# RWKV time mixing: channel pairs transposed as float32 words between the matmuls of R, and a second weight pair

## The chip, the cores and the metric

The kernel runs on one core of a Trainium2 chip. The engines of a core run side by side and wait for each other through semaphores: TensorE (PE, with its weight loads shown apart as PEld), VectorE (DVE), ScalarE (ACT), GpSimd (POOL) and SyncE (SP), beside 16 DMA engines. The metric is the device time of one execution in microseconds (us): the median of several runs.

## The reference

x is 16 batches of 2048 tokens with 256 channels, all float32. Each token is mixed with the token before it, channel by channel, and projected:

```python
x_prev = np.zeros_like(x)
x_prev[:, 1:, :] = x[:, :-1, :].copy()
xv = x * time_mix_v + x_prev * (1 - time_mix_v)
xr = x * time_mix_r + x_prev * (1 - time_mix_r)
v = xv.reshape(-1, d_model) @ value_weight
r = xr.reshape(-1, d_model) @ receptance_weight
r_sigmoid = 1.0 / (1.0 + np.exp(-r))
out = (r_sigmoid * v).reshape(-1, d_model) @ output_weight
```

The key projection of the reference does not reach the output.

## The kernel before

The work is cut into 64 units of 512 tokens, four to a batch. A projection contracts over channels, so x must stand with channels on the 128 partitions: 256 channels make two halves (`ko`). For batches 0 to 9 (`STAGED`; units 0 to 39) TensorE makes that layout: x is loaded as bf16 into `x_bf` (unit 1, and unit 0, as float32 into `x_unit`), and `transposes` turns eight 128x128 blocks of a unit, four token slots by two halves, into one `ps_t` tile of PSUM, of which there are two. ACT copies the tile to `xt`. Batches 10 to 15 reach that layout by DMA transposes (the crossbar) out of a staged bf16 copy in DRAM, and need no work of TensorE for it.

The mixing is split between weights and data: a weight row is scaled by the mix (`tms`), and the data becomes `x + c * x_prev` with `c = 1 / mix - 1` (`c_sb`). The products with c are shared by DVE (`scale`), POOL (`scale_pool`) and ACT (`scale_act`); DVE adds x (`add`). The result is `mix`, with a part for r (m = 0) and one for v (m = 1). `coefficients` makes `tms` and `c_sb` at the start from one transpose of the mix rows.

The schedule is written out by hand. Iteration g of the main loop issues, in this order:

- R: four 512-column matmuls of unit g into `psum_r` (one buffer), by `project`; then ACT's sigmoid into `s_sb`.
- T: `advance` issues the transposes and ACT copies of a later unit, six ahead in the steady state; iterations 2, 5, 6 and 8 take two units (`START_T`). Eight transposes a unit.
- products and sums of later units on DVE; the last sum here releases POOL's product.
- V: four matmuls into `psum_v` (one buffer); DVE's product z = `s_sb` times `psum_v`, into `z_sb`.
- POOL's product (`scale_pool`), and DVE's sum for R of unit g + 2.
- O: eight matmuls of unit g − 1 into `psum_o` (one buffer), ACT's copy to the output tile, and the store.

Each engine takes its instructions in that order. What an iteration waits for are the single PSUM buffers: R for the sigmoid before, V for z before, O for the output copy before, and a transpose for the ACT copy that frees its `ps_t` tile, the tile of two units before. `w_bf` holds both scaled weights for all units; `w_f32` is their float32 source, loaded once at the start.

Of the kernel before, what the change touches and what calls it, by code (L numbers as in the profile page):

```python
# [1 line left out]

# [6 lines left out]
FP32 = mybir.dt.float32  # L9
# [6 lines left out]
def kernel(  # L16
# [47 lines left out]
    ZEROS_AT = 12  # L64
    SINGLE = NU - 6
# [99 lines left out]
    tm_rows = consts.tile([2 * KO, P], FP32)  # L165
    w_f32 = consts.tile([P, 2, KO, D], FP32)
    for m, tm in enumerate([time_mix_r, time_mix_v]):
        nc.scalar.dma_start(
            out=tm_rows[m * KO : (m + 1) * KO, :], in_=tm.rearrange("(ko p) -> ko p", p=P)
        )  # L170

    def load_halves(e):
# [8 lines left out]
        out=w_f32[:, 0], in_=receptance_weight.rearrange("(ko p) n -> p ko n", p=P)  # L181
    )
    load_halves(1)
    nc.sync.dma_start(out=w_f32[:, 1], in_=value_weight.rearrange("(ko p) n -> p ko n", p=P))
# [47 lines left out]
    tm_prev = consts.tile([P, 2, KO], FP32)  # L232

    def coefficients():
        ps = ps_o_pool.tile([P, 2, KO], FP32, name="psum_o")
        nc.tensor.transpose(
            out=ps.rearrange("p m k -> p (m k)"), in_=tm_rows, identity=ident_f[: 2 * KO, : 2 * KO]
        )
# [21 lines left out]
    def transposes(i):  # L260
# [10 lines left out]
        def one(ps, jj, ko, src, idn):  # L271
            nc.tensor.transpose(  # L272
                out=ps[:, jj], in_=src[:, jj, ko * P : (ko + 1) * P], identity=idn
            )

        if i == 1:
            for h in (1, 0):
                ps = ps_t_pool.tile([P, H, KO, P], FP32, name="ps_t")
                for jj in range(H):
                    for ko in range(KO):  # L280
                        one(ps[:, :, ko], jj, ko, x_unit[:, i, h * H : (h + 1) * H], ident_f)
                nc.scalar.copy(out=xt[b][:, j0 + h * H : j0 + (h + 1) * H], in_=ps)
            return
# [5 lines left out]
        nc.scalar.copy(out=xt[b][:, j0 : j0 + UJ], in_=ps)  # L289
        if i in SHIFT_ACT:  # L290
            j, n = (j0 - 1, UJ) if b < BYUNIT else (0, J)
            nc.scalar.copy(out=xt[b][:, j, :, 1:P], in_=xt[b][:, j + n, :, 0 : P - 1])
            shifted.append((b, e))

    def first_transposes():
        def part(lo, n, pool, name):
            ps = pool.tile([P, n, KO, P], FP32, name=name)
            for jj in range(n):
                for ko in range(KO):
                    nc.tensor.transpose(  # L300
                        out=ps[:, jj, ko],
                        in_=x_unit[:, 0, lo + jj, ko * P : (ko + 1) * P],
# [9 lines left out]
        part(1, 1, ps_o_pool, "psum_o")  # L312

# [36 lines left out]

    def scale(piece, kos=(0, 1)):
        b, m, _, _ = piece
        for ko in kos:
# [3 lines left out]
                scalar1=c_sb[:, m, ko : ko + 1],  # L357
# [4 lines left out]
    def scale_pool(piece, after):  # L362
# [4 lines left out]
            scalar1=c_sb[:, m, 1:2],  # L367
# [12 lines left out]
    def project(ps, g, m, lo=0, hi=TU):  # L380
        b, e = divmod(g, UB)
        for mo in range(KO):
            for ko in range(KO):
                nc.tensor.matmul(  # L384
                    out=ps[:, mo, :],
                    lhsT=w_bf[:, m, ko, mo * P : (mo + 1) * P],
# [3 lines left out]
                )  # L390

# [174 lines left out]
    def advance(limit):  # L566
        nonlocal tnext
        while tnext <= min(limit, NU - 1):
            b, e = divmod(tnext, UB)
            for n in LOADS.get((b, e), ()):  # L570
                loads[n] = load(n)
            if tnext < NU - BYDMA:
                transposes(tnext)
            tnext += 1

# [7 lines left out]
    first_transposes()  # L583
# [20 lines left out]
    )  # L604
    scale(pieces(0)[1])
# [43 lines left out]
    def scale_act(piece, kos):  # L649
        b, m, _, _ = piece  # L650
        for ko in kos:
# [4 lines left out]
                scale=c_sb[:, m, ko : ko + 1],  # L656
# [3 lines left out]
    for g in range(NU - 1):  # L660
        ps_r = ps_r_pool.tile([P, KO, TU], FP32, name="psum_r")
        if g == 0:
# [9 lines left out]
        nc.scalar.activation(out=s_sb, in_=ps_r, func=ACT.Sigmoid)  # L672
        advance(START_T[g] if g < len(START_T) else g + LOOK)
# [89 lines left out]
```

## Time and profile before

| what | value |
|---|---|
| median of 3 runs | 199.12 us (198.97 to 199.16) |
| span of the profiled execution | 197.1 us |
| granted TensorE clock, 12 to 180 us | 1.00 in every stretch asked for |
| units with PE transposes, of these with bf16 | 39 after the first, 38 |
| period of a unit with transposes, without | 3.05 us, 2.60 us |
| last bf16 transposes start at | 111.1 us |

The profile's span runs from the first to the last instruction of the program. The profiled execution's own time is not listed apart; what the runs' median has beyond the span, 2.0 us, lies outside the recorded instructions. A row of the timeline has the start, the time to the end of the last instruction merged into it, the engine, the source line, the operation with output and inputs, and the number of instructions. Matmuls overlap their ends with the next one, so distances between starts are what counts on PE.

### The profile page before, as it was taken

Reading aid. Unit: us, or ns where it says so; the run is one execution under the profiler, and the core shown is the slowest. Engines: PE = TensorE matmul, PEld = TensorE weight load, DVE = VectorE, ACT = ScalarE, POOL = GpSimd, SP = SyncE. Lnnn points to the kernel's source line nnn. Section 1 sums busy time; section 2 is a strip of 40 time slices with the busy share of each in tenths; the row PEclk is TensorE's granted clock in tenths of the full one; section 3 lists DMA queues with packets and bytes.
Section 4 is the critical chain, followed back from the end, with each engine's and each line's share of the span. In section 5 each row is a group of like instructions: output and inputs, shape, how many; then the busy total and the mean of one; then the engine's idle time right before and its main releaser. Section 6 shows DMA issues by size and latency. Waiting matters only on the chain.

```text
span 197.1 us, 3735 instructions
## 1 busy us (share of the span) xinstructions
PE 191.8 (97%) x1358; PEld 123.3 (63%) x1364; DVE 183.2 (93%) x286; ACT 177.2 (90%) x197; POOL 85.9 (44%) x117
## 2 busy tenths in 40 slices
PE   8999999999999999999999999999999999999992
PEld 3556676666666666666666666666666666666660
DVE  0999999999999999999999999999999999999962
ACT  3799899999999999999999999999999999999982
POOL 2745542443665635624334266444443444444200
PEclk9999999999999999999999999999999999999999
DMA  5999999999999999999999999999999999999875
GB/s 171 244 190 223 218 263 253 248 264 259 300 419 278 289 294 336 271 236 206 367 206 290 330 347 191 204 210 284 290 301 424 421 419 419 411 422 421 338 321 219
DMA packets 35465, 58.13 MB, mean 295 GB/s; under 512 B 26004, under 2 KB 27000, under 8 KB 30712
## 3 DMA queue, kind: packets, MB, share of 16 engines
q1 hardware_dynamic: 31792, 41.34, 59.8%
q0 software_dynamic: 3504, 16.44, 41.6%
q8 instruction: 10, 0.16, 0.3%
q10 hardware_dynamic: 152, 0.13, 0.2%
q14 instruction: 7, 0.06, 0.1%
HBM read 34.34 MB, written 39.90 MB: 377 GB/s over the span
## 4 chain that ended last, share of the span: by engine, by line
PE 93%; DMA 4%; issue 0%; SPq 0%; ACT 0%
PE psum_r L384 28%; PE psum_v L384 27%; PE psum_o L416 27%; PE ps_t L272 9%; DMA x_bf<-in_x_dram 2%; DMA w_f<-n_receptance_weight_dram 2%; PE ps_t L416 1%; SPq L174 0%; PE psum_v L416 0%; PE ps_t L384 0%; PE psum_r L416 0%; ACT x_bf L446 0%
## 5 line engine op out<-in xcount | busy, mean ns | idle before, releaser
L364 POOL TENSOR_SCALAR mix<-xt_both,c_sb 128x1024 bf16<-128x1024 bf16 (+1 forms) x55 | 61.1, 1110 | 85.6 <-DVE mix L376 82.4
L711 DVE TENSOR_TENSOR z_sb<-s_sb,psum_v 128x1024 bf16<-128x1024 bf16 (+1 forms) x64 | 76.7, 1200 | 2.2 <-PE psum_v L384 1.1
L376 DVE TENSOR_TENSOR mix<-mix,xt_both 128x1024 bf16<-128x1024 bf16 x112 | 76.8, 696 | 1.4
L384 PEld LDWEIGHTS <-w_bf 128*128 128x128 bf16 x512 | 48.5, 98 | 39.1 <-DVE mix L376 0.4
L672 ACT ACTIVATE s_sb<-psum_r 128x1024 bf16<-128x1024 f32 x63 | 65.3, 1036 | 6.2 <-PE psum_r L384 6.0
L384 PE MATMUL psum_v<-mix,w_bf 128*128 128x512 bf16 (+1 forms) x252 | 64.8, 378 | 0.2
L384 PE MATMUL psum_r<-mix,w_bf 128*128 128x512 bf16 x250 | 64.6, 379 | 0.2
L416 PE MATMUL psum_o<-wo_bf,z_sb 128*128 128x256 bf16 x486 | 63.2, 273 | 0.0
L416 PEld LDWEIGHTS <-z_sb 128*128 128x128 bf16 x512 | 51.9, 103 | 17.9 <-DVE z_sb L510 0.7
L471 ACT COPY o_sb<-psum_o 128x1024 f32<-128x1024 f32 x50 | 51.2, 1024 | 4.9 <-PE psum_o L416 4.9
L289 ACT COPY xt_both<-ps_t 128x1024 bf16<-128x1024 bf16 x32 | 32.9, 1039 | 0.0
L272 PEld LDWEIGHTS <-x_bf 128*128 128x128 bf16 x304 | 19.7, 98 | 8.6 <-DMA x_bf<-in_x_dram 1.1
L272 PE MATMUL ps_t<-ident,x_bf 128*128 128x128 bf16 x304 | 22.5, 219 | 0.3 <-DMA x_bf<-in_x_dram 0.3
L354 DVE TENSOR_SCALAR mix<-xt_both,c_sb 128x1024 bf16<-128x1024 bf16 (+1 forms) x47 | 21.3, 463 | 0.0
L652 ACT ACTIVATE mix<-xt_both,c_sb 128x1024 bf16<-128x1024 bf16 x14 | 16.3, 1163 | 0.0
L376 DVE TENSOR_TENSOR mix<-mix,xt_first 128x1024 bf16<-128x1024 bf16 x15 | 10.6, 714 | 0.1
L471 ACT COPY x_bf<-psum_o 128x1024 f32<-128x1024 f32 x10 | 10.2, 1016 | 0.0
L354 DVE TENSOR_SCALAR mix<-xt_first,c_sb 128x512 bf16<-128x512 bf16 x22 | 6.6, 352 | 0.2
L289 ACT COPY xt_first<-ps_t 128x1024 bf16<-128x1024 bf16 x6 | 6.1, 1042 | 0.2 <-PE ps_t L272 0.2
L557 POOL COPY xt_first<-xt_first 128x254 bf16<-128x254 bf16 x5 | 2.0, 392 | 7.2 <-DVE mix L376 5.7
L364 POOL TENSOR_SCALAR mix<-xt_first,c_sb 128x512 bf16<-128x512 bf16 x6 | 4.1, 685 | 1.5 <-DVE mix L376 1.0
L162 POOL DMA_DIRECT2D x_bf<-in_x_dram x8 | 4.7, 583 | 0.0
(68 smaller groups left out, 52.6 us busy)
## 6 DMA issues: line engine op xcount, KB each, us to landing
out_dram<-o_sb SPq DMA_DIRECT2D x25, 1024.0 KB, 11.6
x_bf<-in_x_dram POOLq DMA_DIRECT2D x8, 1024.0 KB, 14.8
x_natural<-in_x_dram POOLq DMA_DIRECT2D x4, 1024.0 KB, 11.8
out_dram<-x_bf SPq DMA_DIRECT2D x4, 1024.0 KB, 14.4
x_natural<-in_x_dram POOLq DMA_DIRECT2D x4, 512.0 KB, 12.6
out_dram<-x_bf SPq DMA_DIRECT2D x4, 512.0 KB, 4.2
x_bf<-in_x_dram POOLq DMA_DIRECT2D x6, 256.0 KB, 6.5
o_sb<-in_x_dram SPq DMA_DIRECT2D x4, 256.0 KB, 3.8
```

Source lines behind the costliest of these rows:

```text
L162: return nc.gpsimd.dma_start(out=x_bf[b], in_=rows(b), max_dma_last_dim=run)
L272: nc.tensor.transpose(out=ps[:, jj], in_=src[:, jj, ko * P : (ko + 1) * P], identity=idn)
L289: nc.scalar.copy(out=xt[b][:, j0 : j0 + UJ], in_=ps)
L354: nc.vector.tensor_scalar(out=mixed(piece, ko), in0=tokens(piece, 0, ko), scalar1=c_sb[:, m, ko : ko + 1], scalar2=None, op0=ALU.mult,)
L364: op = nc.gpsimd.tensor_scalar(out=mixed(piece, 1), in0=tokens(piece, 0, 1), scalar1=c_sb[:, m, 1:2], scalar2=1.0, op0=ALU.mult, op1=ALU.mult,
L376: return nc.vector.tensor_tensor(out=mixed(piece), in0=mixed(piece), in1=tokens(piece, 1), op=ALU.add)
L384: nc.tensor.matmul(out=ps[:, mo, :], lhsT=w_bf[:, m, ko, mo * P : (mo + 1) * P], rhs=mixed((b, m, e * TU + lo, e * TU + hi), ko), start=(k ...
L416: nc.tensor.matmul(out=ps[:, j, :], lhsT=slot[:, ko, j], rhs=wo_bf[:, ko, :], start=(ko == 0), stop=(ko == KO - 1),)
L471: nc.scalar.copy(out=o[:, j0 : j0 + UJ, :], in_=ps)
L652: nc.scalar.activation(out=mixed(piece, ko), in_=tokens(piece, 0, ko), func=ACT.Copy, scale=c_sb[:, m, ko : ko + 1],)
L672: nc.scalar.activation(out=s_sb, in_=ps_r, func=ACT.Sigmoid)
L711: nc.vector.tensor_tensor(out=z_sb[:, :, c : c + n], in0=s_sb[:, :, c : c + n], in1=ps_v[:, :, c : c + n], op=ALU.mult,)
```

## The change

A row of a bf16 token has 256 channels, which are 128 pairs of two bytes each; a pair is read as one float32 word. A transpose of words moves channel 2c to the even half of partition c and channel 2c + 1 beside it, so four float32 transposes do for a unit what eight bf16 ones did, and half `ko` now holds every second channel rather than 128 in a row. ACT's copy reads the two interleaved halves out of PSUM with a step. The weight rows are loaded in that order (`(p ko)` for `(ko p)`), and unit 0 and 1 are transposed with a step of two. The mix rows are transposed in two pieces.

The crossbar keeps the old channel order, so batches from 10 on need weights and coefficients in the old order: `tm_cross` is transposed and copied at the start, and at iteration 10 (`CROSS_AT`) POOL loads both weights again and makes `tms_cross` and `c_cross`, with the reciprocal on DVE. At iterations 20 to 23 POOL scales one weight half each into `w_cross`.

From iteration 3 on (`WEAVE`), the transposes of the later unit are issued between the matmuls of R, one behind each, or two where an iteration takes two units; ACT's copies still stand behind the sigmoid. The diff, cut to its core:

```diff
+    CROSS_AT = 10
+    WEAVE = 3
...
-        out=w_f32[:, 0], in_=receptance_weight.rearrange("(ko p) n -> p ko n", p=P)
+        out=w_f32[:, 0], in_=receptance_weight.rearrange("(p ko) n -> p ko n", p=P)
...
+    def mixes_by(order, pool, name):
+        ps = pool.tile([P, KO, 2], FP32, name=name)
+        rows = tm_rows.rearrange(order, k=KO)
+        for ko in range(KO):
+            nc.tensor.transpose(out=ps[:, ko], in_=rows[:, ko], identity=ident_f[:2, :2])
+        return ps.rearrange("p k m -> p m k")
+
+    def cross_coefficients():
+        nc.gpsimd.tensor_scalar(
+            out=tms_cross, in0=tm_cross, scalar1=0.0, scalar2=1e-30, op0=ALU.is_equal, op1=ALU.mult
+        )
+        nc.gpsimd.tensor_tensor(out=tms_cross, in0=tms_cross, in1=tm_cross, op=ALU.add)
+        nc.vector.reciprocal(c_cross, tms_cross)
+        nc.gpsimd.tensor_scalar(
+            out=c_cross, in0=c_cross, scalar1=-1.0, scalar2=1.0, op0=ALU.add, op1=ALU.mult
+        )
+
+    def load_cross_weights():
+        for m, w in enumerate([receptance_weight, value_weight]):
+            nc.gpsimd.dma_start(out=w_f32[:, m], in_=w.rearrange("(ko p) n -> p ko n", p=P))
...
-        ps = ps_t_pool.tile([P, UJ, KO, P], BF16, name="ps_t")
+        ps = ps_t_pool.tile([P, UJ, P], FP32, name="ps_t")
         src = x_first[:, e - 2] if b == 0 else x_bf[b][:, e * UJ : (e + 1) * UJ, :]
-        for jj in range(UJ):
-            for ko in range(KO):
-                one(ps[:, :, ko], jj, ko, src, ident)
-        nc.scalar.copy(out=xt[b][:, j0 : j0 + UJ], in_=ps)
+        words = src.bitcast(FP32)
+
+        def one(jj):
+            nc.tensor.transpose(out=ps[:, jj], in_=words[:, jj], identity=ident_f)
+
+        def evacuate():
+            nc.scalar.copy(
+                out=xt[b][:, j0 : j0 + UJ],
+                in_=ps.bitcast(BF16).rearrange("p j (c o) -> p j o c", o=KO),
+            )
...
-    def project(ps, g, m, lo=0, hi=TU):
+    def project(ps, g, m, lo=0, hi=TU, between=()):
         b, e = divmod(g, UB)
+        w = w_bf if b < STAGED else w_cross
+        between = list(between)
+        share = -(-len(between) // (KO * KO))
...
+                for one in between[:share]:
+                    one()
+                del between[:share]
...
+        limit = START_T[g] if g < len(START_T) else g + LOOK
+        between, ends = begin(limit) if g >= WEAVE else ([], [])
...
-            project(ps_r, g, 0)
+            project(ps_r, g, 0, between=between)
...
+        if g == CROSS_AT:
+            load_cross_weights()
+            cross_coefficients()
+        if CROSS_AT + 10 <= g < CROSS_AT + 10 + 2 * KO:
+            scale_cross_weight(g - CROSS_AT - 10)
```

How this moves the instructions, at three places. First PE, in an iteration of the steady state, from the last two matmuls of R on; LDWEIGHTS is a weight load, and a float32 transpose has its load in the same row. Before:

```order
L384 LDWEIGHTS w_bf
L384 MATMUL psum_r<-mix,w_bf 128x512
L384 LDWEIGHTS w_bf
L384 MATMUL psum_r<-mix,w_bf 128x512
L272 LDWEIGHTS x_bf
L272 MATMUL ps_t<-ident,x_bf 128x128
```

Now, the same place up to the first matmul of V:

```order
L435 LDWEIGHTS w_bf
L435 MATMUL psum_r<-mix,w_bf 128x512
L321 MATMUL ps_t<-ident_f,x_bf 128x128
L435 LDWEIGHTS w_bf
L435 MATMUL psum_r<-mix,w_bf 128x512
L321 MATMUL ps_t<-ident_f,x_bf 128x128
L435 LDWEIGHTS w_bf
L435 MATMUL psum_v<-mix,w_bf 128x512
```

One transpose stands behind each matmul of R, where eight, each with a load of its own, stood behind the fourth.

Second PE in iteration 6, which transposes units 10 and 11. The rows begin with the transposes behind R's first matmul and go to those behind the fourth; the waits are shown:

```order
L321 MATMUL ps_t<-ident_f,x_bf 128x128 [waits Activation_49]
L321 MATMUL ps_t<-ident_f,x_bf 128x128
L435 LDWEIGHTS w_bf
L435 MATMUL psum_r<-mix,w_bf 128x512
L321 MATMUL ps_t<-ident_f,x_bf 128x128 x2
L435 LDWEIGHTS w_bf
L435 MATMUL psum_r<-mix,w_bf 128x512
L321 MATMUL ps_t<-ident_f,x_bf 128x128 [waits Activation_49]
L321 MATMUL ps_t<-ident_f,x_bf 128x128
L435 LDWEIGHTS w_bf
L435 MATMUL psum_r<-mix,w_bf 128x512
```

Each unit's first transpose waits for the ACT copy of the tile two units before. Both waits stood behind the whole of R and now stand inside it, ahead of its last matmul.

Third POOL and DVE at iteration 10; `z_sb` is z, `mix` a product or a sum. DVE before, from z of iteration 10 to z of iteration 11:

```order
L711 TENSOR_TENSOR z_sb<-s_sb,psum_v 128x1024
L376 TENSOR_TENSOR mix<-mix,xt_both 128x1024
L354 TENSOR_SCALAR mix<-xt_both,c_sb 128x8x128
L376 TENSOR_TENSOR mix<-mix,xt_both 128x1024
L711 TENSOR_TENSOR z_sb<-s_sb,psum_v 128x1024
```

DVE now:

```order
L781 TENSOR_TENSOR z_sb<-s_sb,psum_v 128x1024 [waits PE_49,Activation_49]
L251 RECIPROCAL c_cross<-tms_cross 128x4 [waits Pool_49]
L424 TENSOR_TENSOR mix<-mix,xt_both 128x1024 [waits DVE_49]
L402 TENSOR_SCALAR mix<-xt_both,c_sb 128x8x128
L424 TENSOR_TENSOR mix<-mix,xt_both 128x1024 [waits DVE_49]
L781 TENSOR_TENSOR z_sb<-s_sb,psum_v 128x1024 [waits PE_49,Activation_49]
```

POOL now, from its product of iteration 10 to that of iteration 11, which followed each other directly before:

```order
L412 TENSOR_SCALAR mix<-xt_both,c_sb 128x8x128 [waits DVE_49]
L258 DMA w_f_100<-in_receptance_weight_dram 128x2x256
L258 DMA w_f_100<-in_value_weight_dram 128x2x256 [waits DMAHW7_49]
L247 TENSOR_SCALAR tms_cross<-tm_cross 128x4
L250 TENSOR_TENSOR tms_cross<-tms_cross,tm_cross 128x4 [waits Pool_49]
L252 TENSOR_SCALAR c_cross<-c_cross 128x4 [waits DVE_49]
L412 TENSOR_SCALAR mix<-xt_both,c_sb 128x8x128 [waits DVE_49,PE_49,Activation_49]
```

DVE has a reciprocal more, which waits for POOL's second small operation; that one stands behind two issues of DMAs and the product.

More of the change, by code (lines that the diff above doesn't have):

```diff
@@ L1 @@
 from contextlib import ExitStack
+from functools import partial
 import concourse.bass as bass
@@ L232, with scale_cross_weight @@
     tm_prev = consts.tile([P, 2, KO], FP32)
+    tm_cross = consts.tile([P, 2, KO], FP32)
+    tms_cross = consts.tile([P, 2, KO], FP32)
+    c_cross = consts.tile([P, 2, KO], FP32)
+    w_cross = consts.tile([P, 2, KO, D], BF16)
+    def mixes_by(order, pool, name):
[16 more added lines that the diff above has]
+            nc.gpsimd.dma_start(out=w_f32[:, m], in_=w.rearrange("(ko p) n -> p ko n", p=P))
+    def scale_cross_weight(n):
+        m, ko = divmod(n, KO)
+        nc.gpsimd.tensor_scalar(
+            out=halves(w_cross[:, m, ko, :]),
+            in0=apart(w_f32[:, m, ko, :]),
+            scalar1=tms_cross[:, m, ko : ko + 1],
+            scalar2=1.0,
+            op0=ALU.mult,
+            op1=ALU.mult,
+        )
     def coefficients():
[L235 to L238, printed above, removed]
+        ps = mixes_by("m (p k) -> m k p", ps_o_pool, "psum_o")
         tm = consts.tile([P, 2, KO], FP32)
@@ L312, in first_transposes @@
         part(1, 1, ps_o_pool, "psum_o")
+        return mixes_by("m (k p) -> m k p", ps_t_pool, "ps_t")
     def slots(piece, off=0):
@@ L366, in scale_pool @@
             in0=tokens(piece, 0, 1),
-            scalar1=c_sb[:, m, 1:2],
+            scalar1=coefficient(b, m, 1),
             scalar2=1.0,
@@ L564, with begin @@
     tnext = 1
-    def advance(limit):
+    def begin(limit):
         nonlocal tnext
+        between, ends = [], []
         while tnext <= min(limit, NU - 1):
@@ L572, in advance @@
             if tnext < NU - BYDMA:
-                transposes(tnext)
+                ones, end = transposes(tnext)
+                between += ones
+                ends += [end] if end else []
             tnext += 1
+        return between, ends
+    def advance(limit):
+        between, ends = begin(limit)
+        for step in between + ends:
+            step()
     def apart(row):
@@ L604 @@
     )
+    nc.scalar.copy(out=tm_cross, in_=cross)
     scale(pieces(0)[1])
@@ L655, in scale_act @@
                 func=ACT.Copy,
-                scale=c_sb[:, m, ko : ko + 1],
+                scale=coefficient(b, m, ko),
             )
@@ L669 @@
         else:
-            project(ps_r, g, 0)
+            project(ps_r, g, 0, between=between)
         s_sb = zpool.tile([P, KO, TU], BF16, name="s_sb")
         nc.scalar.activation(out=s_sb, in_=ps_r, func=ACT.Sigmoid)
-        advance(START_T[g] if g < len(START_T) else g + LOOK)
+        for end in ends:
+            end()
+        if g < WEAVE:
+            advance(limit)
         if g in T_AT:
```

41 lines of the change are left out of this document (22 added, 19 removed).

## The prediction

> **What bounds the kernel now.** I read first the busy shares and the chain that ended last, then the table by stretch of time, then the order of events inside one unit.
>
> ```profile
> PE 191.8 (97%) x1358; PEld 123.3 (63%) x1364; DVE 183.2 (93%) x286; ACT 177.2 (90%) x197; POOL 85.9 (44%) x117
> ...
> PE 93%; DMA 4%; issue 0%; SPq 0%; ACT 0%
> ```
>
> PE carries 93% of the chain. DVE and ACT are close behind, so the question for every edit is which of the three it touches. A share over the whole span hides the stages; the table by stretch shows the one with PE transposes (to 111 us):
>
> ```profile
> 60.00:84.00 24.00, 24.00 (x192) 15.84 (x190) 22.94 (x35) 22.37 (x25) 12.58 (x18) 1.00 1.02 295
> 84.00:110.00 26.00, 26.00 (x207) 17.09 (x206) 24.75 (x37) 24.37 (x27) 8.95 (x9) 1.00 1.11 262
> ```
>
> The columns after the length are PE, PEld, DVE, ACT, POOL. PE has no idle at all, at full clock (1.00); DVE is busy for 22.94 of 24.00. A delay put into PE here is never made up, and a saving on PE is worth having only until DVE ends last. One unit on PE:
>
> ```profile
> 62.00 1.03 PE L384 MATMUL psum_r<-mix,w_bf 128*128 128x512 bf16 x4
> 62.87 0.61 PE L272 MATMUL ps_t<-ident,x_bf 128*128 128x128 bf16 x8
> 63.31 1.03 PE L384 MATMUL psum_v<-mix,w_bf 128*128 128x512 bf16 x4
> 64.17 1.04 PE L416 MATMUL psum_o<-wo_bf,z_sb 128*128 128x256 bf16 x8
> 65.05 1.03 PE L384 MATMUL psum_r<-mix,w_bf 128*128 128x512 bf16 x4
> ```
>
> Start to start, R (psum_r) takes 0.87, the eight transposes T 0.44, V 0.86, O 0.88: a period of 3.05 us. Durations overlap, so I use starts only. The same unit on ACT:
>
> ```profile
> 62.20 1.01 ACT L471 COPY o_sb<-psum_o 128x1024 f32<-128x1024 f32 x1 [0.20 <-PE psum_o L416]
> 63.11 1.03 ACT L672 ACTIVATE s_sb<-psum_r 128x1024 bf16<-128x1024 f32 x1
> 64.03 1.02 ACT L289 COPY xt_both<-ps_t 128x1024 bf16<-128x1024 bf16 x1
> ```
>
> One ACT instruction follows another at 0.91. The output copy starts 0.20 after O's slot ends (62.00), so 0.20 is the step from PE to ACT.
>
> **The transposes.** 38 units trade eight bf16 transposes for four float32 ones. The trace has float32 transposes of the same form, on unit 1, at full clock. On PE and on PEld:
>
> ```profile
> 7.18 1.04 PE L272 MATMUL ps_t<-ident_f,o_sb 128*128 128x128 f32 x8
> 8.05 0.59 PE L398 MATMUL psum_r<-xt_first,w_prev 128*128 128x512 bf16 x2
> ```
>
> ```profile
> 6.96 1.01 PEld L272 LDWEIGHTS ps_t<-ident_f,o_sb 128*128 128x128 f32 x8
> 7.94 0.21 PEld L398 LDWEIGHTS <-w_prev 128*128 128x128 bf16 x2
> ```
>
> Eight take 8.05 − 7.18 = 0.87, or 0.109 each, against 0.44 / 8 = 0.055 for a bf16 one. So 4 × 0.109 = 0.436 replaces 0.445: a gain of about 0.01 a unit, 0.3 us over 38 units, as long as a woven one costs as much as one in a row. That is the point to settle. If 0.109 were the weight load, weaving would hide it behind a 512-column matmul. The boundaries speak against it. The first load starts at 6.96, a whole matmul before 7.18, and is hidden already. The last transpose is followed by a bf16 weight load (7.94), which a bf16 transpose hides in 0.055; yet the next matmul starts only at 8.05. With a matmul part of 0.055 the eight would have ended near 7.18 + 7 × 0.107 + 0.055 = 7.98. So the matmul itself takes 0.109, and a woven pair costs 0.216 + 0.109. **Term: −0.3** (−0.4 to −0.2).
>
> The Trainium skill, TensorE: Matmul & The Clock Gate, in the sections on LDWEIGHTS and on the weight-path modes, says that float32 weights get no fast load and that a load takes its columns over 1.2, about 107 ns for 128. By that rule alone the row of eight would be bound by its loads, and weaving would be worth 0.22 us a unit; the step from 7.94 to 8.05 does not agree with it. This is the first rival below.
>
> The reader of the words (ACT, bf16 pairs at a step of 4 bytes) has no row here. The output copy reads float32 at a step of 4 bytes, the present reader bf16 at 2, and both take 1.01 to 1.02; I take no change, and keep the other end, a doubled read (+0.9), for a rival.
>
> **The weave.** From unit 3 on, three of four transposes (six of eight where an iteration takes two units) stand ahead of R's last matmul. In the steady stage R's result comes 0.33 later and the sigmoid starts at 0.20 + 0.87 + 0.33 = 1.40 from the period's start; sigmoid and reader end at 1.40 + 2 × 0.91 = 3.22, and the next output copy is due at 3.04 + 0.20 = 3.24. It just closes, so the steady stage pays nothing; what a longer loop costs is the fourth rival. In the early stage ACT has four or five instructions in some iterations. PE and ACT at iterations 5 and 6:
>
> ```profile
> 23.99 1.03 PE L384 MATMUL psum_r<-mix,w_bf 128*128 128x512 bf16 x4
> ...
> 27.48 1.03 PE L384 MATMUL psum_r<-mix,w_bf 128*128 128x512 bf16 x4
> ```
>
> ```profile
> 25.10 1.03 ACT L672 ACTIVATE s_sb<-psum_r 128x1024 bf16<-128x1024 f32 x1
> 26.01 1.02 ACT L289 COPY xt_both<-ps_t 128x1024 bf16<-128x1024 bf16 x1
> 27.06 0.40 ACT L292 COPY xt_both<-xt_both 128x254 bf16<-128x254 bf16 x1
> 27.37 1.01 ACT L289 COPY xt_both<-ps_t 128x1024 bf16<-128x1024 bf16 x1
> 28.27 1.02 ACT L471 COPY o_sb<-psum_o 128x1024 f32<-128x1024 f32 x1
> ```
>
> In R of iteration 5 the last matmul now ends at 23.99 + 0.87 + 6 × 0.109 = 25.51, so the sigmoid starts at 25.71, not 25.10, and ACT was idle before it. All that follows on ACT is 0.61 later: the reader of unit 9 starts at 27.98 and ends at 28.99. With two ps_t buffers the first transpose of unit 11 waits for that reader. It now stands behind R's third matmul, at 27.48 + 3 × 0.216 + 4 × 0.109 = 28.57, and starts near 29.05: 0.5 us of idle PE, with V and O queued behind it. Carrying ACT on to iteration 10 at 0.91 each, nothing makes this up and little is added. **Term: +0.5** (0, if ACT's lag is swallowed, to 0.9, if a second buffer is caught as well).
>
> **The second weight pair.** At iteration 10 POOL gets, behind its product (scale_pool), two weight loads and two small operations; DVE's reciprocal waits for the second of these, and behind it on DVE stand the sum for R of iteration 12 and the product z of iteration 11. POOL at that place, what such issues cost it elsewhere, and a small POOL operation:
>
> ```profile
> 43.75 1.11 POOL L364 TENSOR_SCALAR mix<-xt_both,c_sb 128x1024 bf16<-128x1024 bf16 x1 [0.98 <-DVE mix L376]
> ```
>
> ```profile
> 79.70 1.11 POOL L364 TENSOR_SCALAR mix<-xt_both,c_sb 128x1024 bf16<-128x1024 bf16 x1 [0.98 <-DVE mix L376]
> 80.77 1.25 POOL L158 DMA_DIRECT2D x_natural<-in_x_dram  x2
> 82.89 1.11 POOL L364 TENSOR_SCALAR mix<-xt_both,c_sb 128x1024 bf16<-128x1024 bf16 x1 [0.87 <-DVE mix L376]
> ```
>
> ```profile
> L554 POOL COPY xt_first<-xt_first 128x2 bf16<-128x2 bf16 x5 | 1.6, 316 | 0.1
> ```
>
> The product ends its slot at 43.75 + 1.07 = 44.82, two issues bring it to about 46.0, two small operations of some 0.2 (0.1 to 0.3) to 46.4. DVE in the same stretch:
>
> ```profile
> 43.57 1.21 DVE L711 TENSOR_TENSOR z_sb<-s_sb,psum_v 128x1024 bf16<-128x1024 bf16 x1
> 44.70 0.70 DVE L376 TENSOR_TENSOR mix<-mix,xt_both 128x1024 bf16<-128x1024 bf16 x1
> ...
> 46.52 1.21 DVE L711 TENSOR_TENSOR z_sb<-s_sb,psum_v 128x1024 bf16<-128x1024 bf16 x1
> ```
>
> The sum that starts at 44.70 now waits to 46.4 plus a reciprocal of about 0.2: DVE loses 1.9 us. The z at 46.52 moves to 48.4 and ends at 49.6. V of the next iteration needs the one psum_v buffer back, as an earlier place shows, where V starts 0.05 after a late z (31.14 + 1.21 = 32.35):
>
> ```profile
> 31.14 1.21 DVE L711 TENSOR_TENSOR z_sb<-s_sb,psum_v 128x1024 bf16<-128x1024 bf16 x1
> ```
>
> ```profile
> 32.40 1.02 PE L384 MATMUL psum_v<-mix,w_bf 128*128 128x512 bf16 x4
> ```
>
> ```profile
> 48.08 1.03 PE L384 MATMUL psum_v<-mix,w_bf 128*128 128x512 bf16 x4
> ```
>
> So the V of 48.08 starts at 49.7. **Term: +1.6** (1.2 with the small operations at 0.1 and issues at 0.55, 2.0 with 0.3 and 0.63); the weave's half microsecond moves both engines and leaves it alone. What goes nowhere: the four weight products on POOL (iterations 20 to 23; estimated at half of a 128x1024 product, 0.55) fit into its idle of at least 0.87 before each product; without it each would cost DVE up to 0.5. The two extra loads, 0.5 MB, run 30 us ahead of their use.
>
> **The start.** Two extra tiny transposes ahead of the coefficients push R of unit 0 by 0.1 to 0.2. Behind it PE waits for a load anyway:
>
> ```profile
> 10.25 0.62 PE L272 MATMUL ps_t<-ident,x_bf 128*128 128x128 bf16 x8 [0.31 <-DMA x_bf<-in_x_dram]
> ```
>
> That load is issued when the first weight lands; the weight now comes in 2 KB pieces, with unknown sign. **Term: +0.1** (−0.3 to +0.4).
>
> **The sum.** −0.3 + 0.5 + 1.6 + 0.1 = +1.9. The profiled execution spans 197.1; the runs' median of 199.12 lies 2.0 above, lead-in that the change does not touch. I expect a span of 199.0 and a time of **201.0**; all terms at their low ends give 199.6, at their high ends 202.2.
>
> **Rivals.**
> 1. The woven transpose costs 0.055, the load having been the limit. PE's period falls to 2.82, but DVE then ends last: 3.05 × 22.94 / 24.00 = 2.91. Saved: 0.13 × 23 iterations (11 to 33) = 3.0; DVE's stall of 1.9 counts in full, weave and start add 0.3: about 198.3. It decides for the other side if a woven transpose takes under some 0.07. For it: nothing here weaves them. Against: the step to 8.05. Chance 0.10.
> 2. The reciprocal hardly bites: if the two load issues did not hold up the POOL operations behind them, the coefficients would be there at 45.3, DVE would lose 0.7 and V 0.4, in all 199.6 or, with the weave free too, 199.2. Against: in the rows above the issues are serial on POOL. Chance 0.12.
> 3. As forecast, 201.0: chance 0.70.
> 4. Reading every second bf16 is slower on ACT. The loop above takes 0.28 more without harm, since the output copy may run into the wait for the sigmoid; a doubled read (+0.9) gives 3 × 0.91 + 0.9 = 3.63 a unit against 3.04, some 17 us over 30 units: 218; half of that, a few microseconds. Chance 0.08.
>
> A measurement of this kernel tells changes over about 0.2% (0.4 us) from none. Faster takes most of rival 1: 0.08. Within 0.2%: the rest of 1 and half of 2: 0.08. Slower: 0.84. The range of 8 in 10 goes from 199.2, which leaves out rival 1, to 202.6, which leaves out rival 4 and takes in the unknown ends.
>
> **What would show it.** Right: R with its woven transposes still 1.30 from start to start of V; a gap on PE of about 1.6 us at V of iteration 12, with DVE's reciprocal waiting for POOL; a gap of about 0.5 in R of iteration 6; a period of 3.04 at 60 to 84 us. Wrong: a period of 2.9 there (rival 1), a DVE that waits under 1 us at the reciprocal (rival 2), or a reader clearly over 1.04 us (rival 4).

## The result and the profile after

| | median | runs | profiled execution | its span |
|---|---|---|---|---|
| before | 199.14 us (198.97 to 200.03) | 4 | not listed apart | 197.1 |
| changed | 201.75 us (201.22 to 201.89) | 4 | 201.22 | 199.4 |

The ratio is 1.0114, with a 95% interval of 1.0077 to 1.0151: slower by 2.6 us in the medians. The profiled execution of the change is its fastest one. Ratios and their intervals, here and below, leave out executions more than 1.5% above the fastest of their kernel; the medians do not.

Three places that the prediction spoke of. First the steady stage, in the table by stretches (per engine busy us and instructions, then granted clock, DMA share, GB/s), of the changed kernel:

```profile
60.00:84.00 24.00, 24.00 (x160) 16.94 (x159) 23.46 (x34) 22.59 (x25) 14.02 (x20) 1.00 1.03 300
```

PE is still busy without a break, with fewer instructions. The groups by line, of the same kernel:

```profile
L321 PE MATMUL ps_t<-ident_f,x_bf 128*128 128x128 f32 x152 | 37.6, 274 | 0.3 <-ACT xt_both L324 0.3
L324 ACT COPY xt_both<-ps_t 128x1024 bf16<-128x1024 bf16 x32 | 32.2, 1015 | 0.0
```

One woven R, at iteration 32, from its second matmul on, and what follows it, on the timeline of PE:

```profile
109.78 0.38 PE L435 MATMUL psum_r<-mix,w_bf 128*128 128x512 bf16 x1
110.00 0.27 PE L321 MATMUL ps_t<-ident_f,x_bf 128*128 128x128 f32 x1
110.11 0.38 PE L435 MATMUL psum_r<-mix,w_bf 128*128 128x512 bf16 x1
...
110.65 0.27 PE L321 MATMUL ps_t<-ident_f,x_bf 128*128 128x128 f32 x1
110.76 1.03 PE L435 MATMUL psum_v<-mix,w_bf 128*128 128x512 bf16 x4
111.92 0.38 PE L435 MATMUL psum_r<-mix,w_bf 128*128 128x512 bf16 x1
...
113.22 1.04 PE L470 MATMUL psum_o<-wo_bf,z_sb 128*128 128x256 bf16 x8
114.09 1.03 PE L435 MATMUL psum_v<-mix,w_bf 128*128 128x512 bf16 x4
114.96 1.03 PE L435 MATMUL psum_r<-mix,w_bf 128*128 128x512 bf16 x4
116.21 1.03 PE L470 MATMUL psum_o<-wo_bf,z_sb 128*128 128x256 bf16 x8 [0.22 <-ACT o_sb L525]
```

From a matmul of R to its transpose are 0.22 us, from there to the next matmul 0.11: a woven float32 transpose costs PE 0.11, and four of them (0.44) as much as the eight bf16 ones did (0.44). ACT reads the interleaved halves in 1015 ns, no slower than the 1039 ns of before. The rows from 110.76 on show something else, the end of the stage with transposes, where O moves from behind V to behind the next R. V's four matmuls take 0.87 of PE, so the next R could start at 111.63 and starts at 111.92; and O at 116.21 waits for ACT.

Second, iteration 6, on the timeline of PE:

```profile
28.12 0.38 PE L435 MATMUL psum_r<-mix,w_bf 128*128 128x512 bf16 x1
28.76 0.44 PE L321 MATMUL ps_t<-ident_f,x_bf 128*128 128x128 f32 x2 [0.26 <-ACT xt_both L324]
```

0.64 us lie between the starts instead of 0.22: the transposes wait for ACT to free a `ps_t` tile, and R, V and O stand behind them. Third, iteration 10, on the timelines of POOL and of DVE:

```profile
44.81 0.78 POOL L258 DMA_DIRECT2D w_f<-n_receptance_weight_dram  x1
45.59 0.73 POOL L258 DMA_DIRECT2D w_f<-in_value_weight_dram  x1
46.40 0.24 POOL L247 TENSOR_SCALAR tms_cross<-tm_cross 128x4 f32<-128x4 f32 x1
46.73 0.20 POOL L250 TENSOR_TENSOR tms_cross<-tms_cross,tm_cross 128x4 f32<-128x4 f32 x1
```

```profile
43.57 1.22 DVE L781 TENSOR_TENSOR z_sb<-s_sb,psum_v 128x1024 bf16<-128x1024 bf16 x1
46.96 0.18 DVE L251 RECIPROCAL c_cross<-tms_cross 128x4 f32<-128x4 f32 x1 [2.17 <-POOL tms_cross L250]
47.06 0.66 DVE L424 TENSOR_TENSOR mix<-mix,xt_both 128x1024 bf16<-128x1024 bf16 x1
...
48.76 1.21 DVE L781 TENSOR_TENSOR z_sb<-s_sb,psum_v 128x1024 bf16<-128x1024 bf16 x1
```

DVE's reciprocal waits 2.17 us behind two issues and two small operations of POOL. The z that started at 46.52 before starts at 48.76, and V of iteration 12, at 48.08 before, at 50.03.

Comparing the starts of R and V of each iteration in both profiles, the change is 0.27 ahead after the start, 0.27 behind after iteration 9, 1.95 behind at V of iteration 12, 1.75 behind at the end of the steady stage, 2.36 behind from iteration 35 on, and stays there. The spans differ by 2.3. The last matmuls of PE in the changed kernel, and the last stretch of its table before the end:

```profile
195.30 0.39 PE L470 MATMUL psum_o<-wo_bf,z_sb 128*128 128x256 bf16 x2
```

```profile
184.00:192.00 8.00, 8.00 (x54) 5.44 (x53) 7.68 (x12) 7.49 (x10) 1.60 (x2) 1.00 0.94 383
```

From the end of that row to the end of the span are 3.75 us; in the kernel before, whose last matmuls end at 193.33, they are 3.78. So far the account closes on PE, with one item, the 0.6 at iterations 32 to 35, that the prediction did not have. The experiments show that it is only half of the account.

### The profile page after: what moved, and what is told of

It reads as the page before. It is cut to its first block, busy times and chain, and to the rows that moved or that the text cites. A ratio compares the mean times of both kernels' runs of the same rounds, so it can differ in the third digit from the quotient of the medians.

```text
span 199.4 us, 3456 instructions
## 1 busy us (share of the span) xinstructions
PE 192.5 (97%) x1215; PEld 126.3 (63%) x1215; DVE 183.9 (92%) x287; ACT 178.0 (89%) x198; POOL 91.8 (46%) x126
## 4 chain that ended last, share of the span: by engine, by line
PE 86%; ACT 5%; DVE 4%; POOL 2%; issue 1%; POOLq 0%
PE psum_v L435 25%; PE psum_o L470 25%; PE psum_r L435 24%; PE ps_t L321 7%; ACT s_sb L739 2%; PE ps_t L205 2%; DVE mix L424 2%; ACT xt_both L324 1%; DVE z_sb L781 1%; PE ps_t L470 1%; ACT o_sb L525 1%; POOL mix L412 1%; POOL w_f L258 1%; DVE mix L402 1%; ACT xt_first L314 1%
## 5 line engine op out<-in xcount | busy, mean ns | idle before, releaser
L412 POOL TENSOR_SCALAR mix<-xt_both,c_sb 128x1024 bf16<-128x1024 bf16 (+1 forms) x31 | 34.3, 1106 | 46.6 <-DVE mix L424 41.6
L435 PEld LDWEIGHTS <-w_bf 128*128 128x128 bf16 x316 | 30.5, 98 | 25.4 <-DVE mix L424 2.5
L412 POOL TENSOR_SCALAR mix<-xt_both,c_cross 128x1024 bf16<-128x1024 bf16 x24 | 27.0, 1124 | 35.4 <-DVE mix L424 34.1
L435 PE MATMUL psum_v<-mix,w_bf 128*128 128x512 bf16 x160 | 41.1, 379 | 1.1 <-DVE z_sb L781 0.8
L321 PE MATMUL ps_t<-ident_f,x_bf 128*128 128x128 f32 x152 | 37.6, 274 | 0.3 <-ACT xt_both L324 0.3
L324 ACT COPY xt_both<-ps_t 128x1024 bf16<-128x1024 bf16 x32 | 32.2, 1015 | 0.0
L435 PEld LDWEIGHTS <-w_cross 128*128 128x128 bf16 x196 | 19.2, 98 | 16.9
L435 PE MATMUL psum_r<-mix,w_cross 128*128 128x512 bf16 x96 | 24.6, 379 | 0.0
L435 PE MATMUL psum_v<-mix,w_cross 128*128 128x512 bf16 (+1 forms) x96 | 24.2, 375 | 0.0
L321 PEld LDWEIGHTS ps_t<-ident_f,x_bf 128*128 128x128 f32 x152 | 20.9, 141 | 4.5 <-ACT xt_both L324 1.4
L717 ACT ACTIVATE mix<-xt_both,c_cross 128x1024 bf16<-128x1024 bf16 x12 | 13.9, 1162 | 0.0
L525 ACT COPY x_bf<-psum_o 128x1024 f32<-128x1024 f32 x10 | 10.2, 1015 | 0.0
```

Of the source, the lines that this page charges most:

```text
L321: nc.tensor.transpose(out=ps[:, jj], in_=words[:, jj], identity=ident_f)
L324: nc.scalar.copy(out=xt[b][:, j0 : j0 + UJ], in_=ps.bitcast(BF16).rearrange("p j (c o) -> p j o c", o=KO),)
L412: op = nc.gpsimd.tensor_scalar(out=mixed(piece, 1), in0=tokens(piece, 0, 1), scalar1=coefficient(b, m, 1), scalar2=1.0, op0=ALU.mult, op1= ...
L435: nc.tensor.matmul(out=ps[:, mo, :], lhsT=w[:, m, ko, mo * P : (mo + 1) * P], rhs=mixed((b, m, e * TU + lo, e * TU + hi), ko), start=(ko = ...
L525: nc.scalar.copy(out=o[:, j0 : j0 + UJ, :], in_=ps)
L717: nc.scalar.activation(out=mixed(piece, ko), in_=tokens(piece, 0, ko), func=ACT.Copy, scale=coefficient(b, m, ko),)
```

## Experiments

Each experiment was timed beside runs of the kernel before, whose medians were 199.06 to 199.20 us; the ratios are against those. "Late" is how much later than in the kernel before (190.32 us) the last unit's first sigmoid starts in the profiled execution, a measure of PE's lateness at the end. T1 and T2 are the two DMA transposes (`by_dma`, in iterations 27 and 39); their ends are those of their rows on SP's queue (the data land some 3 us later). The columns from "late" on are of one profiled execution each, the medians of all.

| kernel | median, us (runs) | ratio, 95% | late | T1 starts | T2 ends | span |
|---|---|---|---|---|---|---|
| before | 199.1 to 199.2 | 1 | 0 | 95.1 | 146.1 | 197.1 |
| changed | 201.75 (4) | 1.0114, 1.0077 to 1.0151 | 2.36 | 96.2 | 148.9 | 199.4 |
| recip_later | 202.03 (6) | 1.0118, 1.0070 to 1.0165 | 1.14 | 96.8 | 147.6 | 198.2 |
| no_weave | 201.70 (6) | 1.0117, 1.0070 to 1.0164 | 1.99 | 97.0 | 150.6 | 201.1 |
| both_undone | 201.38 (5) | 1.0117, 1.0072 to 1.0163 | 2.12 | 97.8 | 148.8 | 199.2 |
| coeff_first | 200.44 (12) | 1.0062, 1.0037 to 1.0088 | 1.52 | 97.7 | 148.6 | 198.6 |
| mix_late | 201.01 (6) | 1.0083, 1.0050 to 1.0117 | 2.02 | 96.9 | 149.6 | 200.2 |
| products_late | 200.47 (12) | 1.0060, 1.0030 to 1.0090 | 1.78 | 97.5 | 149.5 | 200.1 |
| both_late | 201.38 (12) | 1.0110, 1.0080 to 1.0139 | 2.19 | 96.7 | 148.9 | 199.3 |
| no_reload | 201.11 (12) | 1.0064, 1.0029 to 1.0098 | 1.46 | 95.7 | 149.0 | 199.6 |
| before_reload | 200.29 (12) | 1.0052, 1.0022 to 1.0082 | −0.13 | 96.2 | 148.2 | 198.8 |
| undone_no_reload | 200.76 (12) | 1.0067, 1.0038 to 1.0096 | 0.26 | 94.9 | 148.0 | 198.6 |
| shuffle | 201.08 (12) | 1.0071, 1.0035 to 1.0107 | – | – | – | – |
| before_wait | 201.83 (6) | 1.0139, 1.0095 to 1.0184 | 3.01 | 95.7 | 148.5 | 200.1 |

The profile of shuffle is not in the table; it is of an execution of 202.50, far above the median.

### Taking the two engine prices away

recip_later: the reciprocal alone moves to iteration 12, when POOL has long delivered.

```diff
-        nc.vector.reciprocal(c_cross, tms_cross)        # iteration 10
+        if g == CROSS_AT + 2:
+            cross_reciprocal()
```

> The reciprocal of the crossbar coefficients moves from iteration 10 to iteration 12; loads, weave and float32 transposes stay. Theory (the reciprocal's wait for POOL costs PE 1.6 to 1.7 us): about 1.7 us less than the changed kernel, near 200.0 us, no wait at the reciprocal, and no gap on PE at V of iteration 12. Rival (the delay is the extra POOL and DMA work, wherever the reciprocal stands): under 0.5 us less, near 201.5 us.

no_weave: the transposes stay float32, but stand behind R in a block, as before.

```diff
-    WEAVE = 3
+    WEAVE = NU
```

> The four float32 transposes of a unit stand in one block behind R, as the eight bf16 ones did before; all else as in the changed kernel. Theory (the weave costs about 0.5 us at iteration 6 and about 0.6 us where the transposing stage ends, and a transpose costs 0.109 us either way): about 1.1 us less than the changed kernel, near 200.6 us, with the period at 60 to 84 us unchanged at 3.04. Rival (weaving hides the float32 weight load): the period grows, by up to 0.2 us a unit, and the kernel is slower by several us.

both_undone: both edits.

> Reciprocal at iteration 12 and no weave: what is left of the change is the float32 transposes, the reader with a step, and the second weight pair. Theory: the two prices add, 2.8 us less than the changed kernel, 198.7 to 199.1 us, level with the kernel before or 0.3 to 0.5 under it. Rival (the float32 transposes or the reader with a step cost time of their own): it stays over 199.6 us.

coeff_first: the reciprocal stays in iteration 10, but POOL makes the small operations ahead of the two load issues.

```diff
         if g == CROSS_AT:
-            load_cross_weights()
             cross_coefficients()
+            load_cross_weights()
```

> At iteration 10 the coefficient operations are issued ahead of the two weight loads, so POOL reaches them 1.5 us earlier; the reciprocal stays at iteration 10. Theory (DVE waits for POOL's queue, and the two load issues are 1.5 of its 2.2 us): DVE's wait falls to about 0.7 us, and the kernel is about 1.4 us faster than the changed one, near 200.3 us. Rival (the wait is for the coefficient operations themselves or for the transposed mix rows): the wait stays near 2.2 us, and so does the time.

coeff_first did what the mechanism says: the reciprocal waits 0.70 instead of 2.17, PE ends 1.52 late, and the median is 1.3 under the change. The other three are misses. Their profiles show the waits gone as meant: recip_later has no wait of DVE at iteration 10, no_weave none at iteration 6 and a lateness that stays at 1.99 from iteration 31 to the end, without the step of 0.6. Yet all three have a median within 0.4 of the change. (The profiled execution of recip_later, 199.99, is the lowest of its six and lies where the theory put it; that of no_weave, 202.84, is the highest of its six. Of the others there is no profile.) For no_weave a part of the miss is PE's own: it is only 0.37 less late than in the change, not 1.1, because its start was 0.5 later and the reciprocal cost PE 1.99 instead of 1.68. Two more things stood out in the profiles. In both_undone nearly all of PE's lateness is there after two iterations (2.04 of 2.12): R of unit 0 ran at half speed, a matter of that execution's start (last section). And in no_weave the end does not follow PE; here are its last matmuls and the two transposes, on the timelines of PE and SP:

```profile
194.94 0.39 PE L470 MATMUL psum_o<-wo_bf,z_sb 128*128 128x256 bf16 x2
```

```profile
97.03 15.29 SPq L288 DMA_TRANSPOSE xt_both<-x_natural  x1
137.06 13.50 SPq L288 DMA_TRANSPOSE xt_both<-x_natural  x1
```

The kernel before ended 3.8 us behind PE's last work (193.3 to 197.1); this one 5.7 behind (195.3 to 201.1). What ended late were stores, which stand behind T2 in SP's queue; T2 ended 4.4 later than before.

### Three guesses at what is late besides PE

Base of all four is recip_later. mix_late takes the second pair's mix transposes out of the start; products_late lets POOL scale the second pair behind its load issues; both_late does both; no_reload leaves out the two extra loads, so that batches 10 to 15 get weights in the wrong order of channels.

```diff
-        return mixes_by("m (k p) -> m k p", ps_t_pool, "ps_t")    # end of first_transposes
+        if g == CROSS_AT - 3:                                     # mix_late
+            nc.scalar.copy(out=tm_cross, in_=mixes_by("m (k p) -> m k p", ps_t_pool, "ps_t"))
...
-        if CROSS_AT + 10 <= g < CROSS_AT + 10 + 2 * KO:
+        if CROSS_AT + 14 <= g < CROSS_AT + 14 + 2 * KO:           # products_late
...
-            load_cross_weights()                                  # no_reload
```

> Base: the change with its reciprocal moved to iteration 12 (202.03 us median, 199.99 in its profiled execution). Here also the two small float32 transposes of the second pair's mixes, and their copy, leave the start and stand behind iteration 7's woven transposes. Theory A (these transposes among the warm-up matmuls make the TensorE clock rise late, near 9 to 10 us instead of 5, in most executions, for 2 us): the median falls to 199.7-200.4, and in the profile the first pairs of R's matmuls take 0.6 us, not 1.06. Theory B (the second pair's products delay the loads in DRAM, and with them the DMA transposes and the last stores) and theory C (the 0.52 MB that the second pair's loads add are what costs): the median stays at 201.5-202.3.

> Same base (reciprocal at iteration 12); here POOL makes the second pair's four products in iterations 24 to 27 instead of 20 to 23, behind the loads into x_natural that it issues in iterations 22 and 23. Theory B: the first DMA transpose starts at 95.3-96.0 us (base 96.85 with PE 0.5 late; before 95.12) and the second at 134.0-134.6, and the median falls by 0.5-1.5 to 200.5-201.5. Theory A or C: loads move but the median stays at 201.5-202.3.

> Both moves on that base: mixes' transposes out of the start and the four products behind the loads. If A and B together are the whole excess of the base over the kernel before plus weaving's 0.5-1.1: 199.5-200.2 median. If C: not under 201.

> Same base (reciprocal at iteration 12) without the two loads that fetch the weights a second time (the products then scale the rows in the order they were first loaded in, so that batches 10 to 15 are projected with channels in a wrong order). Theory C (their 0.52 MB and POOL's 1.5 us of issuing): the median falls to 199.7-200.5. Theories A and B: it stays at 201.5-202.3, perhaps 0.3 less.

mix_late fell to 201.01, not into the range of theory A, and its profile shows a price of its own: the small transposes take a `ps_t` tile at iteration 7, and PE comes out of iteration 8 some 0.6 later. both_late carries the same price, so its 201.38 beside products_late's 200.47 gives theory A no support; with intervals this wide neither run refutes it. products_late has a median that fits theory B, but not for B's reason: T1 starts at 97.5, no earlier than in the base. no_reload starts T1 at 95.7, 1.2 earlier than the base, as theory C says of the loads, but its time is well above C's range. No single guess explains it. In three of these profiles, though, the span follows T2's end: 149.6 and 200.2, 149.5 and 200.1, 149.0 and 199.6, with PE 2.02, 1.78 and 1.46 late.

### The DMA engines' price alone, and PE's price alone

before_reload is the kernel before with nothing of the change but the two loads, into a tile that nobody reads any more.

```diff
+        if g == 10:
+            for m, w in enumerate([receptance_weight, value_weight]):
+                nc.gpsimd.dma_start(out=w_f32[:, m], in_=w.rearrange("(ko p) n -> p ko n", p=P))
```

> The kernel before, with nothing of the change but the two loads that fetch the weights a second time (0.52 MB, on POOL's queue at iteration 10, into a tile that nothing reads any more). Theory D (the 16 DMA engines are busy without a pause to 184 us, and the first DMA transpose, the second and the last stores follow one another in this traffic; the two loads take 1.1 to 1.5 us of every engine): the first DMA transpose starts at 96.2-96.8 us instead of 95.1, the second ends at 147.3-148.0 instead of 146.1, and the median is 199.9-200.8. Theory of the prediction (only engines that wait for the loads pay): 199.1-199.4, both transposes as before.

This run separates the two best. The transposes on the timeline of SP, of the kernel before and of before_reload:

```profile
95.12 15.38 SPq L254 DMA_TRANSPOSE xt_both<-x_natural  x1
133.82 12.33 SPq L254 DMA_TRANSPOSE xt_both<-x_natural  x1
```

```profile
96.17 15.17 SPq L254 DMA_TRANSPOSE xt_both<-x_natural  x1
134.67 13.54 SPq L254 DMA_TRANSPOSE xt_both<-x_natural  x1
```

PE's last matmuls, in the same order:

```profile
192.94 0.39 PE L416 MATMUL psum_o<-wo_bf,z_sb 128*128 128x256 bf16 x2
```

```profile
192.82 0.39 PE L416 MATMUL psum_o<-wo_bf,z_sb 128*128 128x256 bf16 x2
```

PE is 0.12 early, T1 starts 1.05 late, T2 ends 2.1 late, the span is 1.6 longer and the median 1.2 higher; the interval of the ratio makes that 0.4 to 1.6. T1 and T2 each start 0.1 to 0.2 after the landing of the last load that feeds them. For T1 that load is issued at 81.33 and lands at 95.00 before; with the two extra loads it is issued at 81.23 and lands at 95.98. Of T2's 2.1, though, only 0.85 is its start; 1.2 is its length, and T2 is as long in profiles without the loads (13.3 in undone_no_reload, 13.2 in before_wait). That the loads lengthen it is not shown. T1's start is the clear sign: 94.9 to 95.7 in the four profiles without the loads, 96.2 to 97.8 in the nine with them.

Why half a megabyte matters shows in the table by stretches, first before (its row for 60 to 84 us is in the prediction) and then before_reload:

```profile
184.00:192.00 8.00, 8.00 (x57) 5.65 (x55) 6.42 (x9) 7.27 (x12) 0.89 (x1) 1.00 0.77 314
```

```profile
184.00:192.00 8.00, 8.00 (x58) 5.69 (x57) 6.30 (x9) 7.28 (x12) 0.77 (x1) 1.00 1.01 415
```

From 12 to 184 us the DMA share is 1.0 or above in every stretch, in both kernels. The kernel before has room in it only at the start (0.82 in the first 12 us) and in its last 13 us: 0.77 from 184 to 192. With the two loads the share is 1.01 there, and the stores drain until the end. The loads' half megabyte is 30 us ahead of its use, as the prediction said, but no stretch between shows a lower share in which it could hide. The share alone would not prove that: it can pass 1 (1.18 from 130 to 150 us in before_reload), so it counts some time twice. What shows it is the run.

The Trainium skill, "DMA: Bandwidth & Descriptors", section "Issuing engines are not separate DMA queues", says that DMAs of whatever issuing engine run on the same 16 DMA engines and interleave. This run agrees: a store issued on SP's queue at 44.96 takes 17.6 us to land before, and one at 44.84, beside the loads on POOL's queue, takes 21.5. T1 is no test of it, because the load that it waits for is on POOL's queue as well.

before_wait is the counterpart: a wait of DVE in the place of the change's, and no DMA more.

```diff
+        if g == 10:
+            for _ in range(2):
+                nc.gpsimd.tensor_scalar(out=spare, in0=w_bf, scalar1=c_sb[:, 0, 1:2], scalar2=1.0, op0=ALU.mult, op1=ALU.mult)
+            nc.gpsimd.tensor_scalar(out=tmp, in0=tms, scalar1=1.0, scalar2=1.0, op0=ALU.mult, op1=ALU.mult)
+            nc.vector.reciprocal(rec, tmp)
```

> The kernel before, with nothing of the change but a wait of DVE at iteration 10: POOL makes two products of 128x1024 that nothing reads (2 x 1.12 us) and a 128x4 operation, and a reciprocal that nothing reads waits for it on DVE, where the change's reciprocal stands. No DMA is added. DVE goes on at 47.3-47.4 us instead of 44.7, 2.6 late (2.2 in the change), and TensorE's offset behind iteration 11 is +2.0 to +2.2. If an engine's own price and the DMA engines' price do not add and the later of the two ends the kernel: 201.1-201.6 here, with 200.29 for the two loads alone and 201.75 for the change. If the DMA engines absorb what TensorE loses (they alone set the end): not over 200.3. If the prices add: here 201.1-201.6 too, but then the change should take 199.1 + 1.2 + 2.2 = 202.5.

On its timeline of DVE:

```profile
44.23 1.21 DVE L711 TENSOR_TENSOR z_sb<-s_sb,psum_v 128x1024 bf16<-128x1024 bf16 x1
48.03 0.18 DVE L732 RECIPROCAL rec<-tmp 128x4 f32<-128x4 f32 x1 [2.59 <-POOL tmp L729]
```

A wait of 2.59 makes PE 2.35 later (0.66 to 3.01, the 0.66 being that execution's start), and PE never gets it back. The median, 201.83, is 0.2 over the expected range. Here the DMA share from 184 to 192 us is 0.81, and PE's last matmuls end 3.78 ahead of the span's end, as in the kernel before: PE sets the end. Together, in medians: PE's price alone +2.8 (201.83 − 199.06), the loads alone +1.2 (200.29 − 199.10), and the change, which has both, +2.6 (201.75 − 199.14). The two do not add in full; the later one ends the kernel.

That can be put in numbers. before_reload, which PE does not hold up, ends 50.5 us after T2 (198.76 − 148.21). Let the span be the later of 197.1 plus PE's lateness and T2's end plus 50.5. For the 13 profiles in the table this gives, for instance, 199.5 or 199.4 for the change (199.4), 199.1 or 201.1 for no_weave (201.1), 198.6 or 199.5 for no_reload (199.6), 200.1 or 199.0 for before_wait (200.1), and it is within 0.5 of the span in all 13. The kernel before stands at 197.1 by PE and 196.6 by T2: half a microsecond of room. (The rule takes its 197.1 from the kernel before and its 50.5 from before_reload, so eleven profiles test it. For shuffle's, with T2's end at 150.8 and a span of 200.7, it misses by 0.6.)

Two more figures of the profiles support it. From the end of PE's last matmul to the end of the span are 3.7 to 3.8 us in seven of the 13 (before, changed, recip_later, both_undone, coeff_first, both_late, before_wait): there PE sets the end. In the other six they are 4.8 to 5.7. And after T2's end every profile has 19.3 to 19.4 MB left to move, at 412 to 415 GB/s in the first 36 us, so a late T2 is a late end.

T2's lateness is not the loads' price alone. T2 ends 1.5 to 4.4 later than before in all 12 other profiles, also without the loads: 2.3 in before_wait, 1.8 in undone_no_reload. The last load that feeds T2 is issued by POOL in step with the iterations, at 120.28 before, 122.44 in the change and 123.28 in before_wait. So a late PE makes T2 late as well, and the two bounds are not independent.

### Everything undone, and a cheaper second pair

undone_no_reload is both_undone without the loads; shuffle is both_undone with the second pair moved out of the first one's bf16 rows in SBUF, half the bytes and no products on POOL.

```diff
-            nc.gpsimd.dma_start(out=w_f32[:, m], in_=w.rearrange("(ko p) n -> p ko n", p=P))
+                nc.sync.dma_start(                                # shuffle
+                    out=w_cross[ko::KO, :, h], in_=w_bf[h * n : (h + 1) * n, :, ko]
+                )
```

> The change with nothing woven and the reciprocal at iteration 12 (201.38 us median as it was), and now without the two loads as well (the second pair's products take the rows in the order they were first loaded in, so that batches 10 to 15 are projected with channels in a wrong order). Theory D: all three prices are gone, 198.9-199.6 us, the first DMA transpose at 95.0-95.8. If it stays at 201.0-201.5, the excess of the change is neither weaving, nor the reciprocal, nor the loads, and lies in the float32 transposes' start (two small transposes more, TensorE's clock) or in POOL's products.

> The change with nothing woven, the reciprocal at iteration 12, and the second pair made by four moves from the first pair's bf16 rows in SBUF (0.26 MB on SP's queue at iteration 10) instead of two float32 loads (0.52 MB) and four products on POOL. Theory D: the moves cost some 0.6 us of every DMA engine, half of the loads, so 199.4-200.2 median. If only the engines' own waits counted: 198.9-199.3.

Both miss. undone_no_reload has two of its 12 runs where theory D puts it, 199.08 and 199.16; the other ten lie from 200.24 to 202.27, while of the 29 runs of the kernel before beside it 24 stay under 200. Its profile (an execution of 200.40) has PE 0.26 late and T1 0.25 early:

```profile
94.87 15.23 SPq L290 DMA_TRANSPOSE xt_both<-x_natural  x1
134.64 13.33 SPq L290 DMA_TRANSPOSE xt_both<-x_natural  x1
```

So the loads' price is gone from T1, as D says, but T2 starts 0.8 later than before and takes 1.0 longer, and the span follows T2. shuffle, meant to cost half of what the loads cost, gains nothing that can be measured on both_undone (ratios 1.0071 and 1.0117, with intervals that overlap): 201.08. What in the rest of the change (the start in another order, four products on POOL, weights in another tile) makes T2 late in most executions stays open; T2's length is 12.3 to 13.8 us over the 13 profiles, and no edit here steers it.

One item belongs to the experiments alone: where the reciprocal was moved, DVE's z of iteration 45 starts only as ACT's output copy ends (145.65 and 145.67 in recip_later), and PE loses another 0.3 to 0.4 there. The profile names no releaser, so the cause is not shown.

## Why the prediction was right, and where it was not

The forecast was 201.0, the result 201.75: inside the range, on the right side. The 2.0 us outside the span are nearer 1.8 (201.22 against a span of 199.4); the sum does not depend on it.

**Transposes, −0.3: right.** A woven float32 transpose costs 0.11, and over the 18 iterations from 13 to 31 the sigmoids gain 0.18 on the kernel before, 0.01 a unit. Rival 1, the load as the limit, is out: it wanted a period of 2.9, and the period is 3.04.

**Weave, +0.5: right, but not all.** Iteration 6 costs PE 0.5, through the `ps_t` tile that ACT frees late, as worked out. Missed was the other end of the stage, iterations 32 to 34, where O moves behind the next R. There R waits for a sigmoid that weaving made 0.3 later, the reader and the output copy follow each other on ACT without a gap, and O waits for the copy. That is +0.6, and no_weave, which has neither wait, stays level there. The step that failed is the sum's silence on the end of the woven stage.

**The reciprocal, +1.6: right.** Its wait is 2.17 and PE's loss 1.68. Two deviations cancel in that. DVE loses 2.36, not 1.9 (the sum of 44.70 starts at 47.06), since the two load issues, taken at 0.59 each, need 0.78 and 0.73. And the weave does not leave the term alone: PE is 0.27 late at that place, but DVE's z of iteration 10 starts at 43.57 in both kernels, so some 0.3 of the weave's price lies inside the reciprocal's. Without the weave (no_weave) PE loses 1.99. coeff_first takes two thirds of the wait away and 1.3 of the time (1.0 by the ratios); before_wait makes a like loss, 2.35 for a wait of 2.59, from nothing but a wait, on POOL work instead of issues. Rival 2, a reciprocal that hardly bites, is out.

**"The two extra loads, 0.5 MB, run 30 us ahead of their use": wrong.** They were costed at nothing because no engine waits for them. The runs showed +1.2 for them alone (before_reload; 0.4 to 1.6 by the interval). The cover that the prediction should have named is room on the DMA engines, and by the share there is none from 12 to 184 us. In the change itself this price lies beside PE's and is not paid on top, which is why the forecast came close without it; the prediction had no reason for that, so there it was lucky. The loads are probably one reason why no removal of a wait brought the time back to the kernel before: leaving them out takes 0.9 and 0.6 off the medians (recip_later to no_reload, both_undone to undone_no_reload), though the intervals of the ratios overlap. They are not the only one, as undone_no_reload shows.

**The start, +0.1: mostly within its bounds.** At V of iteration 1 the profiles with the changed start in the table stand between 0.26 early and 0.28 late, and one (both_undone) 2.06 late; by iteration 4 products_late is 0.55 late too. The start of before scatters as much: before_wait has it and is 0.67 late there. In the change's own profile the start is 0.27 early, which covers half of the 0.6 that the sum had missed: luck again.

**Rival 4, a slower reader on ACT: out,** at 1015 ns.

The sum, then, for PE: −0.3 at this start, +0.5, +1.7, −0.2, +0.6, together 2.3. And for the DMA engines: T2 ends 2.8 late, less 0.5 of room, again 2.3. In that execution both arrive within less than the rule can tell; the 3.75 us from PE's end to the span's end say that PE set it. The other three executions of the change, 201.62 to 201.89, have no profile.

The prediction took 0.2% as the least difference that can be told. The intervals above are ±0.25% to ±0.5%, so differences of under half a microsecond between two of these kernels are not shown by the medians.

## What to carry to other kernels

Before a transfer is called hidden, read the DMA share of every stretch between its issue and the end: where that is 1 throughout, as here from 12 to 184 us, expect to pay for it at the end, however early it is issued. The chain of waits will not say so: it follows engines, and in before_reload it still puts 94% on PE while the stores set the end. And where two resources end within half a microsecond of each other, undoing one price shows little; put each price alone into the kernel that has none.

## What the runs showed of the hardware

The start of the program can run at half speed for much longer than usual. In both_undone, on the timeline of PE, against the same place in the changed kernel:

```profile
7.02 1.06 PE L454 MATMUL psum_r<-xt_first,w_prev 128*128 128x512 bf16 x2
7.87 1.06 PE L454 MATMUL psum_r<-xt_first,w_bf 128*128 128x512 bf16 x2
8.72 1.66 PE L313 MATMUL ps_t<-ident_f,o_sb 128*128 128x128 f32 x8
10.22 0.59 PE L454 MATMUL psum_r<-xt_first,w_prev 128*128 128x512 bf16 x2
```

```profile
5.99 0.65 PE L452 MATMUL psum_r<-xt_first,w_prev 128*128 128x512 bf16 x2
6.51 0.61 PE L452 MATMUL psum_r<-xt_first,w_bf 128*128 128x512 bf16 x2
```

From one pair of 512-column matmuls to the next are 0.85 us, and so it goes on to about 10 us, where the changed kernel takes 0.52; the granted clock reads 1.00 throughout. It was one execution of the nine profiled with the changed start (shuffle's counted), none of the three with the start of before or of the two without the small transposes; with so few, that the small transposes cause it is not shown. The Trainium skill, "TensorE: Matmul & The Clock Gate", in its first part on the clock gate, gives 426.7 ns for 512 columns on a cold array and calls the moment at which it warms up variable from run to run; 0.85 for two agrees. It gives about 3.4 us as the time at the lower speed; here that lasts from the first matmuls, at 2.4 us, to about 10.

A POOL product of 128x256 out of float32 took 0.51 us in iteration 20 and 0.92 to 0.93 in the three after it, where the prediction had 0.55 for each. POOL's load issues stand behind two of them (80.09 to 80.96 and 83.10 to 83.96 in the change); that DVE paid for it is not seen.
